# A two-layer hybrid trunk: value products in pairs of key tiles, conditioning sets without deadlines, conditioning groups placed in other gaps, own tiles in the latent chain

## The chip, the cores and the metric

The kernel runs on one core of one Trainium2 chip. The metric is the device time of one execution in microseconds (us). Before the change three runs gave 1645.55, 1646.41 and 1646.59 us (median 1646.41). Engines are called PE (TensorE), DVE (VectorE), ACT (ScalarE), POOL (GpSimd) and SP (the queue that issues most DMAs).

## The reference

Two layers (width 1024) over 256 latent and 256 context tokens. Each layer has a token-mixing half and a convolutional feed-forward half, both between RMS norms, with shift, scale and gate per feature that are computed from a conditioning vector:

```
h  = modulate(x, g0, shift, scale)        # rms_norm(x, g) * (1 + scale) + shift
A  = conv_branch(...)                     # GLU, depthwise conv 31, LayerNorm, swish
B  = window_branch(...)                   # windowed attention, 8 heads, 2 key heads
C  = retention_branch(...)                # two directions, chunks of 128
D  = global_branch(...)                   # attention with normalised q and k
y  = sum_b sigmoid(gate_b(h)) * (branch_b @ w_br[b])
x  = x + gate * rms_norm(y @ w_o)
x  = x + gate' * rms_norm(ConvFFN(modulate'(x)))
```

Attention is `p = softmax(q k^T)`, then `p v`. Latent queries see four key tiles of 128 tokens (two latent, two context), context queries the two of the context. Each layer has 12 conditioning vectors of 1024 (shift, scale and gate of both halves, in half vectors j = 0 to 11 of 512), which are `silu(c) @ ada_w + ada_b`, for latent and for context tokens (v = 0 and 1). Only the latent stream is returned, so layer 1 computes 256 columns where layer 0 computes 512.

## The kernel before

**Products.** Activations lie with features on partitions and tokens in columns. Each large product keeps single precision by splitting both sides in a high and a low part (`hh`, `hl`; `wh`, `wl`) and runs three matmuls per tile: high by high, low by high, high by low. Weights come through SP into `raw` (`NRAW` = 4 buffers); ACT casts `wh`, DVE subtracts to `wl`, and up to `NW` = 6 split units may be live.

**The order.** Nothing reorders the program later: each engine's order is what the Python code emits. A planner decides it while emitting. `Model` keeps a clock per engine and a price per operation (`Engine.us`; the one of a split matmul stands at line 110). `Flow` holds generators in streams (`chain`, `chain2`, `pv`, `main`, `aux`, `fill`, `ada`); after each group of matmuls `poll` advances those whose inputs are ready by the model's clocks and whose stream is not held back by its lag (`STREAMS`). Weight splits are one such piece (`self.weights`). `until(cond)` polls until a condition holds; where nothing can go on, it takes a step of `idle_work`, and otherwise moves the model's PE clock. Since each engine runs its own list in order, an instruction that was put early and waits holds up everything behind it on its engine.

**Value products.** `pv_gen` transposes the softmax weights of a key tile (`ptp`, four transposes), copies them (`PT`, on ACT), and multiplies with the values: `prod(kc)` is two matmuls of 64 stationary columns and 256 moving ones per key tile, which fill the two halves of the partitions of `pv`. One `prod` is emitted per key tile, each after the transposes of the next.

**Conditioning.** It is computed in two ways. `ada_gen` does a half vector on PE: eight products in fp32 (`adp`, 32 stationary columns), a copy on ACT (`adsb`), four transposes (`adt`) and a reduction on DVE. `IDLE` lists the half vectors done so in gaps: after `merge` of layer 0 four, `(0, 10), (0, 11), (1, 10), (1, 11)`; at the end of layer 0 two, `(1, 4), (1, 5)`; in layer 1 none. `ada_stream` does the others on DVE: for each feature block a multiply with reduction over 512 inputs (`adj` for the first vector of a pair, `adw` for the second), two halves. `ADA_SETS` says which half vectors, and at which stage each set begins. Two calls demand the results of a set: `flow.until(ada_need(0, 4, 5))` just before `proj_c`, and `flow.until(ada_need(0, 6, 7, 8, 9))` after the last merge. The first set begins at stage "merge D", the second at "merge A".

**The chain between the halves.** After the output projection `project` (tile `op`, copied to `ys`, squares added up in `Sy`) runs `norm_chain`: a sum over features on PE (`nrm<-ones`), `nv` on DVE, `nr` on POOL, a broadcast on PE (`nrm<-cst_sb,nr`, called R below), then `residual` (per feature block `rt` = gate times R times `ys`, `xs` += `rt`, and for the latent half `q` = square of `xs` on ACT and its sum on PE), again nv, nr, R, then `modulate` (`ht`, `hh`, `hl`). The last feature blocks of the projection are done for the latent half first, so that the latent chain (s = 0) runs beside the context half (s = 1). The tiles `rt`, `q` and `ht` share a ring of four buffers (`half_tmp`). In layer 0 `f` products follow for the latent half, then for the context half; in layer 1 there is only the latent half.

Of the kernel before, what the change touches and what calls it, by code (L numbers as in the profile page):

```python
# [14 lines left out]
D = 1024  # L15
# [12 lines left out]

IDLE = ((((0, 10), (0, 11), (1, 10), (1, 11)), ((1, 4), (1, 5))), ((), ()))

ADA_SETS = (
    ("merge D", 0, (4, 5), (0, 1)), ("merge A", 0, (6, 7, 8, 9), (0, 1)),
    ("ffn", 1, (0, 1, 2, 3), (0, 1)), ("ffn", 1, (6, 7, 8, 9), (0,)),
)
# [4 lines left out]


LEAD = 3

# [55 lines left out]
class Engine:  # L98
# [5 lines left out]
    def us(self, op, out, ins, kw):  # L104
        n = _size(out)
        if self.n == "PE":
            if op == "transpose":
                return 0.123
            if ins[0].dtype == F32R:
                return max(n, 256) / 2400 + 0.002  # L110
            if _size(ins[0]) <= 64:
                return 0.25
            return max(4 * n / 2400, 0.235)
        if self.n == "DMA":
            return max(0.1, 1.43e-3 * n)
        n = max([n] + [_size(x) for x in ins])
        psum = any(x.space == bass.MemoryType.PSUM for x in [out, *ins])
        if self.n == "ACT":
            aps = sum(1 for k in ("scale", "bias") if k in kw and hasattr(kw[k], "shape"))
            return n * 0.833e-3 + (0.05 if psum else 0.093) + 0.093 * aps + (0.06 if "accum_out" in kw else 0)  # L120
        if self.n == "POOL":
            return 0.1 + 0.14 * n
        if op == "reciprocal":
            return 0.06 + 8e-3 * n
        if op == "tensor_tensor_reduce":
            return 0.15 + 1.04e-3 * n
        aps = 0.06 if any(hasattr(kw.get(k), "shape") for k in ("scalar", "scalar1", "scalar2")) else 0
        if op in ("tensor_scalar", "tensor_copy", "memset") and not psum:
            return 0.06 + 0.52e-3 * n + aps
        return 0.065 + 1.04e-3 * n + aps  # L130
# [21 lines left out]
class Flow:  # L152
# [6 lines left out]

    STREAMS = (("chain2", 3.0, 1), ("pv", 3.0, 1), ("main", 1.5, 2), ("aux", 1.5, 1), ("fill", 0.3, 1), ("ada", 0.3, 1))  # L160

    def __init__(self, model):
        self.m = model
        self.post = []
        self.q = {s: deque() for s in ("chain", *(s for s, _, _ in self.STREAMS))}
        self.wait = {}
        self.weights = None
        self.idle_work = deque()

# [41 lines left out]
    def poll(self):  # L211
# [6 lines left out]
        did |= self.advance("chain", 5.0, 1)  # L218
        lim = 1.0 if self.q["chain"] and self.split_ahead() > 2 else 3.0
        if not self.behind(lim) and self.weights():  # L220
            did = True
# [29 lines left out]
def trunk_kernel(  # L251
# [364 lines left out]
    def ada_stream():  # L616
# [8 lines left out]
        for when, l, js, vecs in ADA_SETS:  # L625
            yield (lambda: when in stage,)
            cs = [4 * j + i for j in js for i in range(4)]
            for h in range(2):
                rows_ = [tmp("crow") for _ in vecs]
                for v, r in zip(vecs, rows_):  # L630
                    dma.dma_start(out=r, in_=c_b[:, v, 512 * h:512 * h + 512])
                raw = load(l, cs[0], h)
                for r in rows_:
# [5 lines left out]
                for n_, c in enumerate(cs):  # L639
                    cur, raw = raw, load(l, cs[n_ + 1], h) if n_ + 1 < len(cs) else None  # L640
                    for v, r in zip(vecs, rows_):
# [92 lines left out]
    def residual(l, which, s, ys, b, Sx=None, sums=None):  # L734
# [21 lines left out]
        def add(k, t):  # L756
            dve.tensor_tensor(out=xs[s][k], in0=xs[s][k], in1=t, op=ALU.add)
            if Sx is not None:
                add_sq(Sx, xs[s][k], k == 0)
            if sums is not None:  # L760
                q = half_tmp("q")
                act.activation(out=q, in_=xs[s][k], func=AF.Square)
                sq[k] = q

        for k in range(KD):
            t = half_tmp("rt")
            dve.scalar_tensor_tensor(
# [162 lines left out]
    def pv_gen(br, st, s, c, P):  # L930
# [4 lines left out]
        PT = {}  # L935

        def prod(kc):
            kt = kc + (0 if s == 0 else 2)
            for i in range(2):
# [4 lines left out]
                )  # L944

        for kc in range(nk):
            yield (avail("t"), *(P[q, i] for q in range(2) for i in range(2)))
            pt = bank("t", "ptp")
            for i in range(2):
                for q in range(2):  # L950
                    a = (2 * i + q) * 128
                    pe.transpose(pt[:, a:a + 128], P[q, i][:, kc * 128:kc * 128 + 128], ident)
            if kc:
                if pv is None:
                    yield (avail("v"), PT[kc - 1])
                    pv = bank("v", "pv")
                else:
                    yield (PT[kc - 1],)
                prod(kc - 1)
            yield (pt,)  # L960
# [3 lines left out]
        P.clear()  # L964
        yield (PT[nk - 1],)
        prod(nk - 1)
# [90 lines left out]
    def layer(l, segs):  # L1057
# [354 lines left out]
        def project(which, rh, rl, nk, ys, first, last):  # L1412
# [70 lines left out]
            def chain(s):  # L1483
                yield (lambda: got[s] == KD,)
                yield from norm_chain(l, which, s, ys, Ss[s])

            if last:
# [14 lines left out]
            for m in range(lead, KD):  # L1502
# [7 lines left out]
                else:  # L1510
                    drop()
            for m, w in held:
                p = bank("m", "op")
# [102 lines left out]
        if full:  # L1616
# [14 lines left out]
            flow.drain("aux", "main", "pv")  # L1631
            stage.add("merge D")
            merge(stD)
            flow.until(ada_need(0, 4, 5))
            proj_c()
# [16 lines left out]
        if full:  # L1652
# [3 lines left out]
            merge(stC, last=True)  # L1656
            flow.until(ada_need(0, 6, 7, 8, 9))
        else:
# [43 lines left out]
        if l == 0:  # L1702
            flow.until(ada_need(1, 0, 1, 2, 3, 6, 7, 8, 9))
            for i in IDLE[l][1]:
# [162 lines left out]
```

## Time and profile before

| | |
|---|---|
| Median of 3 runs | 1646.41 us |
| Profiled execution, its own time | 1647.13 us |
| Span of that execution | 1645.3 us |
| PE busy | 1594.7 us (97%) |
| PE weight loads busy | 1349.9 us (82%) |
| DVE busy | 1273.9 us (77%) |
| ACT busy | 796.5 us (48%) |
| Chain that ended last | PE 78%, issue 13%, DVE 5%, DMA 2%, ACT 1% |

Places, in us from the start of the span: input projections of layer 0 to 195; merges of B and D to 372; conv and retention projections (`proj_c`) 374 to 445; merges of A and C to 602; output projection to 652; gap, latent half of `f` 656 to 676; gap, context half from 685; feed-forward to 1041; gap; layer 1 from 1054: mixing to 1398, output projection to 1421, gap to 1441, feed-forward to 1636; end 1645. A row of a timeline has the start, the duration, the engine, the line, the operation with output and inputs, shapes and a count; in brackets the idle time before it and who ended it. Matmuls are pipelined: the distance of two starts says more than the duration shown.

### The profile page before, as it was taken

Reading aid. Unit: us, or ns where it says so; the run is one execution under the profiler, and the core shown is the slowest. Engines: PE = TensorE matmul, PEld = TensorE weight load, DVE = VectorE, ACT = ScalarE, POOL = GpSimd, SP = SyncE. Lnnn points to the kernel's source line nnn. Section 1 sums busy time; section 2 is a strip of 40 time slices with the busy share of each in tenths; the row PEclk is TensorE's granted clock in tenths of the full one; section 3 lists DMA queues with packets and bytes.
Section 4 is the critical chain, followed back from the end, with each engine's and each line's share of the span. In section 5 each row is a group of like instructions: output and inputs, shape, how many; then the busy total and the mean of one; then the engine's idle time right before and its main releaser. Section 6 shows DMA issues by size and latency. Waiting matters only on the chain.

```text
span 1645.3 us, 25202 instructions
## 1 busy us (share of the span) xinstructions
PE 1594.7 (97%) x9430; PEld 1349.9 (82%) x9430; DVE 1273.9 (77%) x2774; ACT 796.5 (48%) x1712; POOL 36.6 (2%) x38
## 2 busy tenths in 40 slices
PE   6999999999999999999999999899999999899998
PEld 3776776787878889888888888788688999799998
DVE  4666897999588774789788766788798976578876
ACT  3666457424432334454344333456666445466653
POOL 0000000000000000000000000000000000000000
PEclk9999999999999999999999999999999999899999
DMA  9411121234533457244544545153133435336552
GB/s 326 169 65 39 65 77 39 77 109 135 186 109 122 159 198 259 70 141 145 177 162 150 186 152 200 56 171 125 46 129 109 154 121 187 128 104 216 183 168 74
DMA packets 84282, 225.87 MB, mean 137 GB/s; under 512 B 9152, under 2 KB 18112, under 8 KB 84160
## 3 DMA queue, kind: packets, MB, share of 16 engines
q1 hardware_dynamic: 83872, 223.74, 40.8%
q8 instruction: 74, 1.21, 0.3%
q10 hardware_dynamic: 288, 0.52, 0.1%
q14 instruction: 48, 0.39, 0.1%
HBM read 223.18 MB, written 1.05 MB: 136 GB/s over the span
## 4 chain that ended last, share of the span: by engine, by line
PE 78%; issue 13%; DVE 5%; DMA 2%; ACT 1%; POOL 0%; SPq 0%; DVEq 0%; POOLq 0%; ACTq 0%
PE mg L136 16%; PE op L136 11%; PE tm L136 11%; PE mb L136 8%; PE fa L136 6%; PE fb L136 6%; PE pv L136 3%; PE sc L136 2%; PE pg L136 2%; PE pa L136 2%; PE ptp L136 2%; PE f L136 2%; PE cqk L136 1%; PE co L136 1%; PE csc L136 1%
## 5 line engine op out<-in xcount | busy, mean ns | idle before, releaser
L136 DVE TENSOR_TENSOR wl<-raw,wh 128x512 fp32r<-128x512 f32 (+1 forms) x624 | 403.7, 679 | 106.9 <-ACT wh L136 105.6
L136 ACT CAST wh<-raw 128x512 fp32r<-128x512 f32 (+1 forms) x624 | 358.1, 613 | 174.7 <-PE fb L136 46.3
L136 PE MATMUL mg<-hh,wh 128*128 128x512 f32 (+1 forms) x512 | 179.0, 350 | 0.0
L136 PE MATMUL mg<-hh,wl 128*128 128x512 f32 (+1 forms) x512 | 172.2, 336 | 0.0
L136 PE MATMUL mg<-hl,wh 128*128 128x512 f32 (+1 forms) x512 | 172.2, 336 | 0.0
L136 DVE SCALAR_TENSOR_TENSOR co<-zp,hdw,co 128x482 f32<-128x482 f32 (+29 forms) x240 | 129.9, 600 | 0.0
L136 PE MATMUL op<-gh,wh 128*128 128x256 f32 (+1 forms) x382 | 124.8, 327 | 0.0
L136 PE MATMUL op<-gh,wl 128*128 128x256 f32 (+1 forms) x382 | 123.5, 323 | 0.0
L136 PE MATMUL op<-gl,wh 128*128 128x256 f32 (+1 forms) x382 | 123.5, 323 | 0.0
L136 PE MATMUL tm<-wh,hh 128*128 128x512 f32 x272 | 112.6, 414 | 3.8 <-ACT hh L136 2.8
L136 PEld LDWEIGHTS mg<-hh,wh 128*128 128x128 f32 x512 | 97.0, 189 | 21.7 <-issue 13.4
L136 PE MATMUL tm<-wl,hh 128*128 128x512 f32 x272 | 107.7, 396 | 3.2 <-DVE wl L136 3.2
L136 PE MATMUL tm<-wh,hl 128*128 128x512 f32 x272 | 107.7, 396 | 1.8 <-DVE hl L136 1.8
L136 PEld LDWEIGHTS mg<-hh,wl 128*128 128x128 f32 x512 | 97.0, 190 | 10.3
L136 PE MATMUL fa<-hh,wh 128*128 128x256 f32 (+1 forms) x312 | 104.6, 335 | 0.0
L136 PE MATMUL fa<-hh,wl 128*128 128x256 f32 (+1 forms) x312 | 104.4, 335 | 0.0
L136 PE MATMUL fa<-hl,wh 128*128 128x256 f32 (+1 forms) x312 | 104.4, 335 | 0.0
L136 PE MATMUL fb<-hh,wh 128*128 128x256 f32 (+1 forms) x312 | 104.4, 335 | 0.0
L136 PE MATMUL fb<-hl,wh 128*128 128x256 f32 (+1 forms) x312 | 104.4, 335 | 0.0
L136 PE MATMUL fb<-hh,wl 128*128 128x256 f32 (+1 forms) x312 | 104.4, 335 | 0.0
L136 ACT ACTIVATE mth<-mg 128x512 f32<-128x512 f32 (+1 forms) x64 | 31.4, 490 | 150.2 <-PE mg L136 149.8
L136 PEld LDWEIGHTS mg<-hl,wh 128*128 128x128 f32 x512 | 97.2, 190 | 8.2
(251 smaller groups left out, 3766.0 us busy)
## 6 DMA issues: line engine op xcount, KB each, us to landing
raw<-in_w_fm SPq DMA_DIRECT2D x88, 512.0 KB, 3.5
raw<-in_f_up SPq DMA_DIRECT2D x88, 512.0 KB, 3.6
adw<-in_ada_t SPq DMA_DIRECT2D x112, 256.0 KB, 4.0
adw<-in_ada_w SPq DMA_DIRECT2D x80, 256.0 KB, 5.6
raw<-in_w_tm SPq DMA_DIRECT2D x40, 512.0 KB, 3.5
raw<-in_w_br SPq DMA_DIRECT2D x32, 512.0 KB, 3.8
raw<-in_f_d SPq DMA_DIRECT2D x32, 512.0 KB, 3.5
raw<-in_w_o SPq DMA_DIRECT2D x16, 512.0 KB, 3.9
```

The lines of the kernel that those rows point to most:

```text
L136: r = f(*a, **kw)
```

## The change

1. `pv_gen` emits the products of two key tiles together, after the transposes of the third; the last two after the loop. 2. `ADA_SETS`: the first set begins at "merge A" instead of "merge D"; both `flow.until(ada_need(0, ...))` calls are gone; the last set loses half vector (1, 6); loads run three ahead instead of one; the lag of stream `ada` goes from 0.3 to 1.0. 3. `IDLE`: (1, 10) and (1, 11) go from layer 0's middle gap to layer 1's; (1, 6) joins the end of layer 0. 4. In `residual` with sums each block has an own tile `rq`, whose first half holds the update and whose second half the square. 5. `flow.hot`: from the end of the last projection's first part until the latent chain is done, weight splits are held back while the chain or a post step is due within 0.6 us. 6. The model's price of a split matmul rises by about 0.011 us.

```diff
--- before.py
+++ after.py
@@ -26,11 +26,11 @@
 
 MERGE_ORDER = ((1, 3, 0, 2), (1, 3, 2, 0))
 
-IDLE = ((((0, 10), (0, 11), (1, 10), (1, 11)), ((1, 4), (1, 5))), ((), ()))
+IDLE = ((((0, 10), (0, 11)), ((1, 4), (1, 5), (1, 6))), (((1, 10), (1, 11)), ()))
 
 ADA_SETS = (
-    ("merge D", 0, (4, 5), (0, 1)), ("merge A", 0, (6, 7, 8, 9), (0, 1)),
-    ("ffn", 1, (0, 1, 2, 3), (0, 1)), ("ffn", 1, (6, 7, 8, 9), (0,)),
+    ("merge A", 0, (4, 5), (0, 1)), ("merge A", 0, (6, 7, 8, 9), (0, 1)),
+    ("ffn", 1, (0, 1, 2, 3), (0, 1)), ("ffn", 1, (7, 8, 9), (0,)),
 )
 NT = 60
 NRAW = 4
@@ -38,6 +38,7 @@
 NW = 6
 
 
+AHEAD = 3
 LEAD = 3
 
 
@@ -107,7 +108,7 @@
             if op == "transpose":
                 return 0.123
             if ins[0].dtype == F32R:
-                return max(n, 256) / 2400 + 0.002
+                return (max(n, 256) + 32) / 2400
             if _size(ins[0]) <= 64:
                 return 0.25
             return max(4 * n / 2400, 0.235)
@@ -157,7 +158,7 @@
 
 
 
-    STREAMS = (("chain2", 3.0, 1), ("pv", 3.0, 1), ("main", 1.5, 2), ("aux", 1.5, 1), ("fill", 0.3, 1), ("ada", 0.3, 1))
+    STREAMS = (("chain2", 3.0, 1), ("pv", 3.0, 1), ("main", 1.5, 2), ("aux", 1.5, 1), ("fill", 0.3, 1), ("ada", 1.0, 1))
 
     def __init__(self, model):
         self.m = model
@@ -165,6 +166,7 @@
         self.q = {s: deque() for s in ("chain", *(s for s, _, _ in self.STREAMS))}
         self.wait = {}
         self.weights = None
+        self.hot = False
         self.idle_work = deque()
 
     def now(self):
@@ -217,6 +219,8 @@
                     self.post.remove(g)
         did |= self.advance("chain", 5.0, 1)
         lim = 1.0 if self.q["chain"] and self.split_ahead() > 2 else 3.0
+        if self.hot and self.split_ahead() > 0 and (self.soon("chain", 0.6) or any(self.there(g, 0.6) for g in self.post)):
+            lim = -9.0
         if not self.behind(lim) and self.weights():
             did = True
         for s, lim, width in self.STREAMS:
@@ -629,7 +633,7 @@
                 rows_ = [tmp("crow") for _ in vecs]
                 for v, r in zip(vecs, rows_):
                     dma.dma_start(out=r, in_=c_b[:, v, 512 * h:512 * h + 512])
-                raw = load(l, cs[0], h)
+                raw = deque(load(l, c, h) for c in cs[:AHEAD])
                 for r in rows_:
                     yield (r,)
                     th = tmp("crth")
@@ -637,7 +641,9 @@
                     yield (th,)
                     dve.scalar_tensor_tensor(out=r, in0=th, scalar=1.0, in1=r, op0=ALU.add, op1=ALU.mult)
                 for n_, c in enumerate(cs):
-                    cur, raw = raw, load(l, cs[n_ + 1], h) if n_ + 1 < len(cs) else None
+                    cur = raw.popleft()
+                    if n_ + AHEAD < len(cs):
+                        raw.append(load(l, cs[n_ + AHEAD], h))
                     for v, r in zip(vecs, rows_):
                         yield (cur, r)
                         o = ada[l][:, c, v:v + 1]
@@ -758,12 +764,17 @@
             if Sx is not None:
                 add_sq(Sx, xs[s][k], k == 0)
             if sums is not None:
-                q = half_tmp("q")
+                q = both[k][:, 256:512]
                 act.activation(out=q, in_=xs[s][k], func=AF.Square)
                 sq[k] = q
 
+        both = {}
         for k in range(KD):
-            t = half_tmp("rt")
+            if sums is None:
+                t = half_tmp("rt")
+            else:
+                both[k] = tmp("rq")
+                t = both[k][:, 0:256]
             dve.scalar_tensor_tensor(
                 out=t, in0=ys[k][:, half(s)], scalar=gain[l][:, (1, 3)[which], k, s:s + 1], in1=R,
                 op0=ALU.mult, op1=ALU.mult,
@@ -943,6 +954,10 @@
                     PT[kc][:, 256 * i:256 * i + 256], start=(kc == 0), stop=(kc == nk - 1),
                 )
 
+        def prods(kcs):
+
+            yield (avail("v"), *(PT[kc] for kc in kcs)) if pv is None else tuple(PT[kc] for kc in kcs)
+
         for kc in range(nk):
             yield (avail("t"), *(P[q, i] for q in range(2) for i in range(2)))
             pt = bank("t", "ptp")
@@ -950,19 +965,20 @@
                 for q in range(2):
                     a = (2 * i + q) * 128
                     pe.transpose(pt[:, a:a + 128], P[q, i][:, kc * 128:kc * 128 + 128], ident)
-            if kc:
-                if pv is None:
-                    yield (avail("v"), PT[kc - 1])
-                    pv = bank("v", "pv")
-                else:
-                    yield (PT[kc - 1],)
-                prod(kc - 1)
+            if kc == 2:
+                yield from prods((0, 1))
+                pv = bank("v", "pv")
+                prod(0)
+                prod(1)
             yield (pt,)
             PT[kc] = tmp("PT")
             act.copy(PT[kc], pt)
             free(pt)
         P.clear()
-        yield (PT[nk - 1],)
+        yield from prods((nk - 2, nk - 1))
+        if pv is None:
+            pv = bank("v", "pv")
+        prod(nk - 2)
         prod(nk - 1)
         yield (pv,)
         yh, yl = st["yh"][c][:, half(s)], st["yl"][c][:, half(s)]
@@ -1483,6 +1499,8 @@
             def chain(s):
                 yield (lambda: got[s] == KD,)
                 yield from norm_chain(l, which, s, ys, Ss[s])
+                if s == 0:
+                    flow.hot = False
 
             if last:
                 hready.clear()
@@ -1509,6 +1527,8 @@
                     held.append((m, w))
                 else:
                     drop()
+            if last and not end:
+                flow.hot = True
             for m, w in held:
                 p = bank("m", "op")
                 chunks([(p, w)], rh, rl, half(1), nk)
@@ -1629,9 +1649,7 @@
             go("main", *attention("D", stD, segs))
             merge(stB, first=True)
             flow.drain("aux", "main", "pv")
-            stage.add("merge D")
             merge(stD)
-            flow.until(ada_need(0, 4, 5))
             proj_c()
             go("main", ret_start(), *(ret_gen(h) for h in range(4)))
         else:
@@ -1654,7 +1672,6 @@
             merge(stA, there=lambda: not flow.q["fill"])
             flow.drain("main")
             merge(stC, last=True)
-            flow.until(ada_need(0, 6, 7, 8, 9))
         else:
             merge(stC, there=lambda: not flow.q["main"])
             merge(stA, last=True, there=lambda: not flow.q["fill"])
@@ -1700,7 +1717,7 @@
                     down(gi - 1, ys)
         flow.drain("aux")
         if l == 0:
-            flow.until(ada_need(1, 0, 1, 2, 3, 6, 7, 8, 9))
+            flow.until(ada_need(1, 0, 1, 2, 3, 7, 8, 9))
             for i in IDLE[l][1]:
                 flow.idle_work.append(ada_gen(*i, ada_load(*i)))
         down(2, ys)
```

**PE, merges of layer 0.** `mg` is the gate product of a merge, `pv` the value products, `sc` scores of the next head pair. Before:

```order
L136 MATMUL mg<-hh,wh 128x512
L136 MATMUL mg<-hl,wh 128x512
L136 MATMUL mg<-hh,wl 128x512
L136 MATMUL pv<-PT,kv 64x256 x2
L136 MATMUL mg<-hh,wh 128x512
L136 MATMUL mg<-hl,wh 128x512
L136 MATMUL mg<-hh,wl 128x512
L136 MATMUL pv<-PT,kv 64x256 x2
L136 MATMUL mg<-hh,wh 128x512
L136 MATMUL mg<-hl,wh 128x512
L136 MATMUL mg<-hh,wl 128x512
L136 MATMUL ptp<-cst_sb,P 128x128 x4
```

The same stretch of the merge after the change:

```order
L137 MATMUL mg<-hh,wh 128x512
L137 MATMUL mg<-hl,wh 128x512
L137 MATMUL mg<-hh,wl 128x512
L137 MATMUL pv<-PT,kv 64x256 x4
L137 MATMUL mg<-hh,wh 128x512
L137 MATMUL mg<-hl,wh 128x512
L137 MATMUL mg<-hh,wl 128x512
L137 MATMUL ptp<-cst_sb,P 128x128 x4
L137 MATMUL sc<-KT,QT 128x256 x8
```

Two bursts of two matmuls have become one of four, and the transposes of the tiles stand by themselves.

**DVE, conv and retention projections (`proj_c`) of layer 0.** `adj` and `adw` are the reductions of the first conditioning set, the rows with `ada_93 128x1` read the sum, `wl` are the low parts of the weights of `proj_c`, `CG` its gate. Before, the end of the set and what follows:

```order
L136 ISA adw,ada_93<-adw,crow,ada_93 128x512
L136 ISA ada_93 128x1
L136 SCALAR_TENSOR_TENSOR gain_95<-ada_93,vec_sb 128x8
L136 TENSOR_TENSOR wl<-raw,wh 128x512 x22
L136 SCALAR_TENSOR_TENSOR CG<-cth,tm 128x512
```

After the change, the rows there:

```order
L137 SCALAR_TENSOR_TENSOR av<-ath,av 128x512
L137 SCALAR_TENSOR_TENSOR yAl<-av,yAh 128x512
L137 TENSOR_TENSOR wl<-raw,wh 128x512 x16
L137 SCALAR_TENSOR_TENSOR CG<-cth,tm 128x512
L137 TENSOR_TENSOR CG<-CG,gn 128x512
L137 SCALAR_TENSOR_TENSOR CG<-cth,tm 128x512
```

The 32 reductions of that set, which all stood ahead of the 22 `wl` before, now stand among the merges of A and C.

**PE, middle gap of layer 1.** `op` is the end of the output projection, `nrm` the norm's sums (from `Sy`, then from `q` or `rq`) and broadcasts (from `nr`), `xtp` transposes of `xs` for the end of the kernel, `f` the first products behind the gap. Before:

```order
L136 MATMUL op<-ah,wh 128x256
L136 MATMUL op<-al,wh 128x256
L136 MATMUL op<-ah,wl 128x256
L136 MATMUL nrm<-ones,Sy 128x1 x2
L136 MATMUL nrm<-cst_sb,nr 128x128 x2
L136 MATMUL nrm<-ones,q 128x1 x16
L136 MATMUL xtp<-cst_sb,xs 128x128 x4
L136 MATMUL nrm<-cst_sb,nr 128x128 x2
L136 MATMUL f_14378<-hh,wh 128x256
L136 MATMUL f_14378<-hl,wh 128x256
```

After the change:

```order
L137 MATMUL op<-ah,wl 128x256
L137 MATMUL adp<-adw,cS 32x512 x4
L137 MATMUL nrm<-ones,Sy 128x1 x2
L137 MATMUL adp<-adw,cS 32x512 x4
L137 MATMUL nrm<-cst_sb,nr 128x128 x2
L137 MATMUL adp<-adw,cS 32x512 x8
L137 MATMUL nrm<-ones,rq 128x1 x12
L137 MATMUL adt<-cst_sb,adsb 128x128 x4
L137 MATMUL nrm<-ones,rq 128x1 x4
L137 MATMUL adt<-cst_sb,adsb 128x128 x4
L137 MATMUL nrm<-cst_sb,nr 128x128 x2
L137 MATMUL f_14350<-hh,wh 128x256
```

The sixteen products and eight transposes of two conditioning half vectors stand in the gap, between the chain's steps; the `xtp` have gone behind the first `f` products.

## Rows read from the trace of the kernel before

**Rows 1.** The page, part 1: busy time, share of span, count of instructions.

```profile
PE 1594.7 (97%) x9430; PEld 1349.9 (82%) x9430; DVE 1273.9 (77%) x2774; ACT 796.5 (48%) x1712; POOL 36.6 (2%) x38
```

**Rows 2.** Timeline of PE in merge D of layer 0: a value burst.

```profile
235.43 0.40 PE L136 MATMUL mg<-hh,wl 128*128 128x512 f32 x1
235.76 0.65 PE L136 MATMUL pv<-PT,kv 128*64 128x256 f32 x4
...
236.68 0.39 PE L136 MATMUL mg<-hl,wh 128*128 128x512 f32 x1
236.91 0.39 PE L136 MATMUL mg<-hh,wl 128*128 128x512 f32 x1
```

**Rows 3.** Tile pv: duration min/median/max in ns, first and last start.

```profile
L136 PE MATMUL pv<-PT,kv x320: 379/404/431, 113.9 to 1264.8; 128*64 128x256 f32 x160
```

**Rows 4.** Timeline of PE, start of the kernel: conditioning products of 256 columns.

```profile
32.37 1.07 PE L136 MATMUL adp<-adw,cS 128*32 128x256 f32 x16 [0.27 <-DVE ada L136]
...
39.09 0.64 PE L136 MATMUL adp<-adw,cS 128*32 128x256 f32 x8
```

**Rows 5.** Timeline of DVE in proj_c of layer 0: two of the reductions.

```profile
405.41 0.75 DVE L136 CUSTOM_DVE_ANT_0 adj<-adw,crow,ada 128x512 f32<-128x512 f32 x1
...
406.88 0.75 DVE L136 CUSTOM_DVE_ANT_0 adj<-adw,crow,ada 128x512 f32<-128x512 f32 x1
```

**Rows 6.** Timeline of PE in proj_c of layer 0.

```profile
407.19 0.39 PE L136 MATMUL tm<-wh,hh 128*128 128x512 f32 x1
...
410.75 0.79 PE L136 MATMUL tm<-wl,hh 128*128 128x512 f32 x1 [3.18 <-DVE wl L136]
...
414.25 0.39 PE L136 MATMUL tm<-wh,hh 128*128 128x512 f32 x1
```

**Rows 7.** Windows: busy us (instructions) of each engine, clock, DMA share, GB/s.

```profile
445.00:602.00 157.00, 156.19 (x735) 126.12 (x733) 131.82 (x308) 52.10 (x92) 4.93 (x4) 1.00 0.41 139
1329.00:1332.00 3.00, 3.00 (x15) 3.00 (x16) 1.32 (x5) 0.38 (x1) 0.70 (x1) 0.50 0.00 0
1421.00:1441.00 20.00, 11.80 (x48) 10.30 (x48) 11.85 (x28) 6.21 (x15) 1.77 (x2) 0.59 0.33 114
```

**Rows 8.** Timeline of PE, middle of layer 0.

```profile
654.33 0.71 PE L136 MATMUL nrm<-cst_sb,nr 128*128 128x128 f32 x4 [0.98 <-POOL nr L136]
...
656.15 0.38 PE L136 MATMUL f<-hh,wh 128*128 128x256 f32 x1 [1.11 <-ACT hh L136]
...
676.31 2.78 PE L136 MATMUL adp<-adw,cS 128*32 128x512 f32 x24
...
685.14 0.39 PE L136 MATMUL f<-hh,wh 128*128 128x256 f32 x1 [1.11 <-ACT hh L136]
...
705.80 1.03 PE L136 MATMUL adt<-cst_sb,adsb 128*128 128x128 f32 x8
...
709.88 0.49 PE L136 MATMUL fa<-hh,wh 128*128 128x512 f32 x1
```

**Rows 9.** Timeline of PE and ACT, end of layer 0.

```profile
1053.76 1.11 PE L136 MATMUL adt<-cst_sb,adsb 128*128 128x128 f32 x4 [3.86 <-ACT adsb L136]
...
1053.14 0.56 ACT L136 COPY adsb<-adp 128x512 f32<-128x512 f32 x1
```

**Rows 10.** Timeline of ACT and DVE, middle of layer 1.

```profile
1421.19 1.14 ACT L136 CAST wh<-raw 128x512 fp32r<-128x512 f32 x2
...
1427.97 0.47 DVE L136 SCALAR_TENSOR_TENSOR rt<-ys,gain,nrm 128x256 f32<-128x256 f32 x1
...
1434.64 0.48 DVE L136 SCALAR_TENSOR_TENSOR rt<-ys,gain,nrm 128x256 f32<-128x256 f32 x1 [0.44 <-PE nrm L136]
```

**Rows 11.** Timeline of DVE, middle of layer 0: the same step beside the projection.

```profile
642.51 0.48 DVE L136 SCALAR_TENSOR_TENSOR rt<-ys,gain,nrm 128x256 f32<-128x256 f32 x1
...
644.21 0.48 DVE L136 SCALAR_TENSOR_TENSOR rt<-ys,gain,nrm 128x256 f32<-128x256 f32 x1
```

**Rows 12.** Timeline of PE, end of retention in layer 1.

```profile
1328.31 0.30 PE L136 MATMUL cyt<-cst_sb,cy 128*128 128x128 f32 x1 [2.17 <-DVE cy L136]
```

## The prediction

> **What bounds the kernel now.** I read the page's first part: PE is busy 97% of the span, DVE 77% [rows 1]. So time can only go by less PE work per result, or by closing the few stretches where PE waits or runs at half clock. I looked for these with the timeline of PE, stage by stage, from waits to what they leave behind: a wait costs twice, because the granted clock falls behind it. In [rows 6] PE waits for a low half of weights between 407.19 and 410.75, then needs until 414.25 for eight products (0.44 each) that elsewhere start 0.23 apart [rows 2]. The windows view confirms it where retention ends in layer 1 (clock 0.50, that is 1.2 of 2.4 GHz) and in layer 1's middle gap (0.59) [rows 7].
>
> **Value bursts.** In [rows 2] the stream product before a burst starts at 235.43, the second one behind it at 236.68: 1.25 us for two stream products at 0.23 and the burst, so 0.79 for two matmuls (four rows). Their 0.65 from first start to last end, less the 0.40 that one lasts [rows 3], puts the two halves 0.25 apart; 0.50 of the 0.79 is work, 0.29 is paid once per burst. There are 320 rows of value products [rows 3], 80 bursts. The order after has 40 bursts of twice the size, so 40 are saved: 40 x 0.29 = 11.6 us. The nearest other row: conditioning products of the same 256 columns, sixteen rows 1.07 against eight 0.64 [rows 4]; 0.43 for what a second key tile adds would give 40 x 0.36 = 14.4. The other end is nothing, if each key tile pays its own entry. I take 11.6, from the row of the operation itself.
>
> These bursts use 64 stationary columns between products of 128. The Trainium skill (TensorEngine Tiling (Array Packing), Key Properties under Tiling Modes) says that changing the tiling mode drains the engine while changing the tile within a mode does not. By it the fixed part is paid once per burst and the sum keeps the 11.6; if each pair of tiles drained by itself, the term would be 0, a rival below. No row of before has a value burst of four, so the trace leaves that open.
>
> **The first conditioning set.** Before, its 32 reductions stand in front of the weight halves of the retention projection, demanded by the call ahead of it. Two take 406.88 - 405.41 = 1.47, so 0.735 each [rows 5]. PE pays 410.75 - 407.19 - 0.23 = 3.33 for the wait and 3.50 - 8 x 0.23 = 1.66 for the half clock [rows 6]: 5.0 us. In the order after no reduction stands there. Bounds: 5.0 if the wait goes, 0 if the next late thing (casts, weights) takes its place; I take 5.0, since PE waits there for DVE alone.
>
> These reductions go into the merges of A and C: the order has 84 there, 56 before, so 28 x 0.735 = 20.6 us more. DVE is busy 131.8 of the 157 us there [rows 7], which leaves 25.2: it fits, with 4.6 to spare, and PE has no slack in it (156.2 busy). Since no call demands the results at once any more, a reduction can be put where the model sees DVE ahead. Cover gone would mean late weight halves. Bounds 0 and +6 (a wait as in [rows 6] with its half clock, once); I take +2.
>
> **Middle of layer 0.** Four things. (a) The latent chain's broadcast R now stands twelve products ahead of the projection's end; before it came at 654.33 [rows 8], some two us behind it (the list of places has its end at 652), so with twelve products at 0.12 and its own length the chain is some 4 us earlier. (b) But the weight splits are held back until the chain is done, and on ACT the copy of the conditioning product stands behind all eight `hh`, with the transposes on PE waiting for it ahead of `f`. That pattern is in the trace at the end of layer 0: 3.86 us of waiting [rows 9]. The chain's gain is therefore lost on its way to `f` and `f` starts later by about as much: +4.0. (c) The gap ahead of the context half, 676.31 to 685.14 = 8.8 us [rows 8], holds sixteen products of conditioning and transposes between the chain's steps; they are gone from there, and the context chain runs ahead while `f` waits. I leave 4 us for the norm and the modulation: -4.8. (d) The conditioning burst at 705.80 to 709.88 goes: -4.1. Sum -4.9; -8.9 if the held splits cost nothing, +4 if the gap refills.
>
> **End of layer 0.** One half vector more. Its copy (0.56, [rows 9]) and four transposes stand behind the `hh`, +1.0, and three splits stand before the first `ht`, +0.5: +1.5. Bounds -2 (the copies now come in two parts, the first early) and +4 (a second wait like 3.86).
>
> **Middle of layer 1.** From the third to the eighth `rt`, 1427.97 to 1434.64, five steps take 6.67 us, each waiting for PE to release one of four shared buffers [rows 10]. With own tiles the step is as beside the projection in layer 0, 1.70 for two [rows 11]; 5 x 0.85 = 4.25, so -2.4. The last square of `ys` stands behind two casts of 1.14 [rows 10], which are now held back: -1.1. The conditioning products fill PE's idle time between the chain's steps; if they hold the clock, the broadcasts and sums go at full speed, worth about 1.0 (a broadcast of four rows 0.71 in [rows 8], and the window's clock is 0.59 [rows 7]). The four transposes of `xs` that leave the gap now cost PE time in the stream: half of the eight transposes in 1.03 at 705.80 [rows 8], +0.5, less a little of the gap they leave: +0.4. Sum -4.1. Late results are the other bound: sixteen products at 24 rows in 2.78 [rows 8] (two rows each) are 3.7 us, 7.4 at half clock, beside a gap of 20: +3 if half of that lands on the chain or on their loads, which SP now issues ahead of the feed-forward's weights. -8 if all of PE's half clock goes.
>
> Here the skill speaks against the change: TensorE: Matmul & The Clock Gate (Part 4: PE-mode transpose) says that transposes don't count as PE being busy. By it the eight transposes ahead of `f` hold nothing, the 1.0 is lost and the term is -3.1. The trace shows a gap with transposes and broadcasts before 685.14 [rows 8], without telling transposes apart.
>
> **End of retention, layer 1.** PE waits 2.17 for DVE at 1328.31 [rows 12], then three us at clock 0.50 [rows 7], half of them lost: 3.7. Before, the product that needs these transposes stands right behind; after, 132 instructions lie between. I take -3.7; bounds -5 and +3 (the transposes wait elsewhere).
>
> **Sum.** -11.6 - 5.0 + 2.0 - 4.9 + 1.5 - 4.1 - 3.7 = -25.8. The profiled execution took 1647.13 (span 1645.3), so 1621.3; the median of the runs lies 0.7 below it, 1620.6. I say 1621.
>
> **Rivals.** *Bursts give nothing* (each key tile pays its 0.79): 1621.3 + 11.6 = 1633. For it: no row shows four in a burst. Against: eight more conditioning rows in one burst cost 0.43 and not 0.64 [rows 4]. *The gaps don't close*: chains in the three gaps and the end of retention find another late step, and only bursts and the first set stay: 1647.1 - 11.6 - 5.0 + 2.0 = 1632.5. For it: each gap ends in a wait of 1.11 for `hh` [rows 8] that nothing changes, and every chain still goes through POOL. *DVE binds the merges of A and C* and the kernel is slower: each added reduction delays a weight half, PE waits 20.6 us and half as much again goes at half clock, as 1.66 followed 3.33 in [rows 6]: 30.9 instead of 2.0. The rest is -27.8, so +3.1: 1650. It decides from 18.5 us of waits on. Against it stand the 25.2 idle us of DVE [rows 7]; for it, that they come in pieces, and that the order is fixed by a model. *Both of the first two at once*: 1632.5 + 11.6 = 1644, which can't be told from no change.
>
> **Numbers.** Forecast 0.56 (own range 1612 to 1630), gaps stay 0.20, bursts nothing 0.13, both 0.05, slower 0.06. The measurement can tell 0.2% (3.3 us) from no change. Faster 0.89, same 0.05, slower 0.06. The unknown bounds below (14.4 for the bursts, -8.9 and -8 for the gaps) reach 1611 without all meeting; above, both middle rivals with some loss reach 1638. Range 1611 to 1638.
>
> **What would show it.** Value bursts of four whose distance between the stream products around them is about 1.3 us net, not 1.58; no wait of PE for `wl` and full clock in the retention projection; DVE some 152 busy of 157 in the merges of A and C with PE still without waits; `rt` steps of 0.85 in layer 1 instead of 1.3; the context half of `f` within 5 us behind the latent one; no burst of 4 us behind it. Wrong would be waits for `wl` in the merges beyond 5 us in sum, a conditioning copy that holds `f` by over 6 us, or bursts of four at twice the price.

## The result, and the profile after

The changed kernel takes 1627.91 us (median; 1625.57 to 1629.71), the kernel before 1646.5 in the same runs: ratio 0.9887, interval 0.987 to 0.9904, 18.6 us faster. The forecast was 1621 with a range of 1611 to 1638: direction and range held, the gain was 7 us smaller. The profiled execution of after took 1629.71 (span 1627.9, 17.4 shorter than before). The page's first part of after, against [rows 1]:

```profile
PE 1583.5 (97%) x9450; PEld 1356.1 (83%) x9450; DVE 1263.4 (78%) x2762; ACT 791.1 (49%) x1711; POOL 35.8 (2%) x38
```

By stage, from PE's timelines (from the start of the last product of one stage to that of the next, so the gap ahead of a stage counts with it):

| Stretch | before | after | difference |
|---|---|---|---|
| start to the end of merges B and D | 372.0 | 364.1 | -7.9 |
| conv and retention projections, with the gap ahead | 72.6 | 67.1 | -5.4 |
| merges of A and C | 157.8 | 168.7 | +10.9 |
| output projection | 49.6 | 51.1 | +1.5 |
| gap, `f`, to the last product ahead of the first `op` of the feed-forward | 133.9 | 130.1 | -3.8 |
| rest of layer 0, its end gap, layer 1's first projection | 294.5 | 293.7 | -0.8 |
| from there to the end of layer 1's merges | 317.1 | 307.7 | -9.4 |
| output projection, middle gap, the 480 products of `f`, `fa`, `fb` | 104.4 | 101.7 | -2.7 |

The first stretch differs by itself between profiles: after, e10 and e12, whose program for PE is the same up to there, have 363.3 to 365.2. Two things stand out: nearly every term has the forecast's sign, and one stage gave 10.9 us back. PE's timeline of after at a value burst, to be held against [rows 2]:

```profile
231.47 0.40 PE L137 MATMUL mb<-yh,wl 128*128 128x512 f32 x1
231.79 1.08 PE L137 MATMUL pv<-PT,kv 128*64 128x256 f32 x8
232.81 0.50 PE L137 MATMUL mg<-hh,wh 128*128 128x512 f32 x1
233.14 0.40 PE L137 MATMUL mg<-hl,wh 128*128 128x512 f32 x1
```

233.14 - 231.47 = 1.67 us with the burst, less two stream products at 0.23: 1.21 for four products (eight rows), where two bursts of two cost 1.58.

The retention projection, where PE had waited 3.3 us and run slowly [rows 6], is full (windows view of after: PE busy 43.00 of 43.00, clock 1.00):

```profile
388.00:431.00 43.00, 43.00 (x191) 35.63 (x190) 12.85 (x21) 13.06 (x24) 0.00 (x0) 1.00 0.34 115
```

The merges of A and C are not. Windows view of after, then of before, of this stage (span, busy us and counts of PE, weight loads, DVE, ACT, POOL, clock, DMA share, GB/s):

```profile
431.50:600.00 168.50, 160.90 (x737) 129.59 (x735) 148.35 (x358) 51.79 (x96) 5.15 (x4) 0.98 0.47 155
```

```profile
444.80:602.60 157.80, 156.99 (x737) 126.81 (x737) 132.62 (x309) 52.27 (x93) 4.93 (x4) 1.00 0.41 138
```

PE has 7.6 us without work where it had 0.8, with the same 737 rows; DVE still has 20 us free. So DVE is not full, but late. PE's timeline of after, the waits of this stage:

```profile
441.69 1.14 PE L137 MATMUL csc<-CQK 64*128 64x256 f32 x8
...
447.00 1.13 PE L137 MATMUL csc<-CQK 64*128 64x256 f32 x4
...
450.15 1.05 PE L137 MATMUL co<-tmo,scD 128*128 128x128 f32 x8
...
454.05 0.71 PE L137 MATMUL co<-tmo,scD 128*128 128x128 f32 x4 [2.84 <-DVE scD L137]
...
491.01 1.95 PE L137 MATMUL co<-tmo,scD 128*128 128x128 f32 x16
...
507.59 0.33 PE L137 MATMUL cyt<-cst_sb,cy 128*128 128x128 f32 x1 [3.11 <-DVE cy L137]
```

The score products `csc` of the chunk come in bursts, two of them at 441.69 and 447.00; `co` waits 2.84 for the decayed scores `scD`, later `cyt` 3.11 for `cy`, and behind each wait stream products start 0.43 apart instead of 0.23: half clock. DVE's timeline of after shows why they are late:

```profile
441.88 0.49 DVE L137 TENSOR_TENSOR E<-E,cst_sb 128x128 f32<-128x128 f32 x2
...
448.16 0.69 DVE L137 SCALAR_TENSOR_TENSOR scD<-csc,E 128x512 f32<-128x512 f32 x1 [5.79 <-PE csc L137]
...
486.15 0.68 DVE L137 SCALAR_TENSOR_TENSOR crow<-crth,crow 128x512 f32<-128x512 f32 x1
...
492.55 0.75 DVE L137 CUSTOM_DVE_ANT_0 adj<-adw,crow,ada 128x512 f32<-128x512 f32 x1 [5.71 <-PE co L137]
```

DVE stands idle for 5.79 and for 5.71 us, each time for PE. The second of these rows decides how to read both: a reduction `adj` reads loads and earlier sums, nothing that PE writes, yet it waits for PE's `co` (the burst at 491.01). It can only wait for its own buffer. All these tiles share one pool of 60 buffers (`NT`), and a tile takes one whose last reader has been emitted, run or not; in the built program that `adj` has the buffer of an `scD` which `co` still reads, and the `scD` of the first row, whose scores were done with the burst at 441.69, has the buffer of a `CQK` tile that the last `csc`, at 447.00, still reads. `tmp` takes buffers without telling the planner who held them, so the planner's model knows nothing of such waits.

### The profile page after: what moved, and what is told of

Read it like the earlier page. It is cut to its first block, busy times and chain, and to the rows that moved or that the text cites. A ratio compares the mean times of both kernels' runs of the same rounds, so it can differ in the third digit from the quotient of the medians.

```text
span 1627.9 us, 25230 instructions
## 1 busy us (share of the span) xinstructions
PE 1583.5 (97%) x9450; PEld 1356.1 (83%) x9450; DVE 1263.4 (78%) x2762; ACT 791.1 (49%) x1711; POOL 35.8 (2%) x38
## 3 DMA queue, kind: packets, MB, share of 16 engines
q8 instruction: 74, 1.21, 0.3%
## 4 chain that ended last, share of the span: by engine, by line
PE 75%; issue 13%; DVE 8%; DMA 2%; ACT 1%; SPq 0%; POOL 0%; DVEq 0%; POOLq 0%; ACTq 0%
PE mg L137 15%; PE op L137 11%; PE tm L137 11%; PE mb L137 7%; PE fa L137 6%; PE fb L137 6%; PE f L137 2%; PE pv L137 2%; PE pa L137 2%; PE pg L137 2%; PE sc L137 2%; PE ptp L137 2%; DVE wl L137 2%; PE cqk L137 1%; DMA adw<-in_ada_w 1%
## 5 line engine op out<-in xcount | busy, mean ns | idle before, releaser
L137 DVE TENSOR_TENSOR wl<-raw,wh 128x512 fp32r<-128x512 f32 (+1 forms) x624 | 404.0, 680 | 104.4 <-ACT wh L137 103.5
```

Source lines behind the costliest of these rows:

```text
L137: r = f(*a, **kw)
```

## The experiments

Times are medians, before 1646.0 to 1646.4 in each group of runs. "A and C" is the length of those merges in the run's profile, from their first product to their last (157.6 before, 168.5 after).

| Run | Time | Ratio to before, interval | A and C | loads ahead |
|---|---|---|---|---|
| e1_bursts_only | 1639.37 | 0.9957, 0.9943 to 0.997 | 157.7 | 1 |
| e2_no_bursts | 1642.28 | 0.9978, 0.9968 to 0.9988 | 169.5 | 3 |
| e3_deadlines_back | 1633.72 | 0.9923, 0.991 to 0.9935 | 167.1 | 3 |
| e4_early_no_deadline | 1625.80 | 0.9877, 0.9863 to 0.989 | 168.6 | 3 |
| e5_before_bursts_lag | 1638.01 | 0.9947, 0.9935 to 0.996 | 155.8 | 1 |
| e6_before_bursts_price | 1634.96 | 0.9926, 0.9914 to 0.9939 | 158.4 | 1 |
| e7_lag_back | 1633.37 | 0.9921, 0.9907 to 0.9934 | 159.1 | 1 |
| e8_lag_back_early | 1615.16 | 0.981, 0.9797 to 0.9823 | 156.1 | 1 |
| e9_one_ahead_early | 1616.35 | 0.9822, 0.9809 to 0.9836 | 157.8 | 1 |
| e10_no_hold | 1622.70 | 0.9857, 0.9844 to 0.9871 | 168.3 | 3 |
| e11_best_no_hold | 1610.40 | 0.9784, 0.9769 to 0.9798 | 156.1 | 1 |
| e12_shared_ring | 1638.47 | 0.9954, 0.9941 to 0.9966 | 169.0 | 3 |

### What the bursts are worth

**e1_bursts_only** is the kernel before with the new `pv_gen`, **e2_no_bursts** the changed kernel with the old one.

```diff
 # e1: before with
-            if kc: ... prod(kc - 1)
+            if kc == 2: yield from prods((0, 1)); ...; prod(0); prod(1)
 # e2: the same, undone in after
```

> The kernel before with the value products in bursts of two key tiles and nothing else of the change. In the profile after, a burst of four products costs 1.22 us net where two bursts of two cost 2 x 0.79. Theory: 40 bursts saved at 0.36 each, -14.4 us against the kernel before, about 1632. The forecast's size (0.29 each, -11.6): 1635. Rival, that the bursts only shift the waits of softmax: 1643 or more.

> The changed kernel with one value product per key tile as before. Theory: the 14.4 us come back, about 1642. Rival, that part of the saving belongs to the other edits (a merge that runs with fewer interruptions meets its weights late): 1634 or less.

Taken from the changed kernel the bursts cost 1642.3 - 1627.9 = 14.4, as the theory had it. Put into the kernel before they brought only 6.8. PE's timeline of e1 shows where the rest stayed:

```profile
365.26 1.03 PE L136 MATMUL atp<-cst_sb,co 128*128 128x128 f32 x8
...
372.32 3.78 PE L136 MATMUL abc<-cst_sb,arr 128*128 128x128 f32 x16 [6.03 <-POOL arr L136]
...
375.76 0.77 PE L136 MATMUL cqk<-hh,wh 128*128 128x512 f32 x1
```

The merge of D, now shorter, ends before the conv branch's norm is done: PE waits 6.03 us for it, then starts `cqk` at half clock. The gap ahead of that projection is 10.7 us here, 2.4 before, 1.0 after the whole change. In part it is made good at once: DVE catches up meanwhile (the first set's reductions end 3.6 us earlier than before), the wait for `wl` of [rows 6] is gone without any edit to the conditioning, and the projections take 66.1 us instead of 70.2. So 14.4 is the worth of the bursts only where what stands ahead of the next stage is early too; e6 below shows which part of the change brings that about.

### What slows the merges of A and C

**e3_deadlines_back** and **e4_early_no_deadline** are the changed kernel with the first set begun at merge D again, e3 with both deadlines, e4 without.

```diff
-    ("merge A", 0, (4, 5), (0, 1)),
+    ("merge D", 0, (4, 5), (0, 1)),
+            stage.add("merge D")          # ahead of merge(stD)
+            flow.until(ada_need(0, 4, 5)) # e3 only, and the one for 6 to 9
```

> The changed kernel with the first conditioning set begun at merge D again and both deadlines in place (loads three ahead and the lag stay as changed). Theory: the merges of A and C, which took 168.5 us after against 157.7 before, are slowed by the reductions that stand between the retention's steps on DVE; with the set gone from there they take 157 to 160, and the retention projection pays about 5 again: about 1622 to 1624, faster than the changed kernel. Rival, that the merges are slow because the planner's new price or lag places the retention's products worse: merges stay at 168, about 1632.

> The changed kernel with the first conditioning set begun at merge D again, but without the deadlines: its reductions fill DVE's free time from merge D on. Theory: merges of A and C 157 to 160 us and no wait in the retention projection: about 1618. Rival (the planner's price or lag): merges stay at 168, about 1628. A third: DVE's reductions delay weight halves in the conv and retention projections without a deadline too: about 1622.

The theory fell: with 64 reductions in the stage (56 before the change, 79 in the changed kernel) it still took 167.1 and 168.6. The deadlines cost 7.9 us between e3 and e4, and the wait for `wl` goes with them and not with the set's place: the projections take 70.3 us in e3, 66.9 in e4. What was left were the lag, the price and the loads ahead, which I had not named.

**e5_before_bursts_lag** and **e6_before_bursts_price** are e1 with one of the planner's numbers each; **e7_lag_back** and **e8_lag_back_early** are the changed kernel and e4 with the lag and the loads as before.

```diff
 # e5: e1 with                            # e6: e1 with
-("ada", 0.3, 1)                          -max(n, 256) / 2400 + 0.002
+("ada", 1.0, 1)                          +(max(n, 256) + 32) / 2400
 # e7: after, e8: e4, each with
-AHEAD = 3                                -("ada", 1.0, 1)
+AHEAD = 1                                +("ada", 0.3, 1)
```

> The kernel before with the value bursts (1639.4 alone) and the lag of stream ada at 1.0 instead of 0.3. The first set with or without its deadline left the merges of A and C at 167 to 169 us, so neither its reductions nor its place slows them. Theory: the lag does; with it reductions are emitted while the model sees DVE up to 1.0 us ahead of PE, so they stand in front of the retention's decay products on DVE. Merges of A and C 166 to 169, about 1648. Rival (the price of a split matmul): they stay at 158, about 1639.

> The kernel before with the value bursts and the new price of a split matmul, lag 0.3. Theory (the lag): merges of A and C 157 to 160, about 1639. Rival (the price): 166 to 169, about 1648.

> The changed kernel with the lag at 0.3 and one conditioning load ahead, as before the change; sets, price, gaps, hold and tiles stay. Theory (the lag): the merges of A and C fall from 168.5 towards 158, fewer reductions fit in there, and the kernel takes about 1618. Rival (the price): 168 and 1628. A third, that the reductions which no longer fit in land where the output projection's chain needs DVE: 158, but 1624 or more.

> The changed kernel with the lag at 0.3, one load ahead, and the first set begun at merge D without deadlines (1625.8 with the lag at 1.0). Theory: merges of A and C near 158, no wait in the retention projection: 1615 to 1617. Rival (the price): 1626.

Neither number slows the stage by itself (155.8, 158.4). But e6 answers what e1 left open. PE's timeline of e6 where e1 waited 6.03 us:

```profile
365.40 1.95 PE L136 MATMUL abc<-cst_sb,arr 128*128 128x128 f32 x16
367.10 0.48 PE L136 MATMUL cqk<-hh,wh 128*128 128x512 f32 x1
```

With the new price added to e1, and nothing else, PE no longer waits for the norm, the gap ahead of the projection is 1.9 us, and the kernel is 4.4 us faster than e1, though the wait for `wl` is back (3.7 in the waits view). So the sixth edit, for which the forecast has no term, carries part of the bursts' gain.

e7 and e8 heal the stage (159.1, 156.1). They changed two things together, though, lag and loads. e8 is 10.6 us faster than e4. e7 is no gain: with the stage healed its conditioning comes too late for the middle gap of layer 0 (ten reductions stand on DVE between 661.3 and 669.4 us, ahead of the `ht` that `f` needs), the waits view of PE there having (wait in total, times, longest):

```profile
PE nrm L137 <- DVE Sx L137: 13.1, 1, 13.1
PE f L137 <- ACT hh L137: 5.4, 1, 5.4
```

**e9_one_ahead_early** separates lag and loads: e4 with one load ahead, lag at 1.0.

```diff
-AHEAD = 3
+AHEAD = 1
```

> The changed kernel with the first set begun at merge D without deadlines, one load ahead, and the lag left at 1.0: the fast variant (1615.2) with only the lag as changed. Theory (the lag together with the new price slows the retention): merges of A and C 167 to 169, about 1626. Rival (the three loads ahead did it): 156 to 159, about 1616.

The rival is right: 1616.35, the stage at 157.8. Windows view and DVE's timeline of e4, then of e9, for the same stage:

```profile
430.90:599.60 168.70, 162.80 (x737) 130.32 (x736) 138.68 (x328) 52.22 (x93) 5.46 (x4) 0.97 0.40 134
```

```profile
441.25 0.48 DVE L137 TENSOR_TENSOR E<-E,cst_sb 128x128 f32<-128x128 f32 x2
...
447.54 0.69 DVE L137 SCALAR_TENSOR_TENSOR scD<-csc,E 128x512 f32<-128x512 f32 x1 [5.81 <-PE csc L137]
...
490.59 0.75 DVE L137 CUSTOM_DVE_ANT_0 adj<-adw,crow,vec_sb 128x512 f32<-128x512 f32 x1 [4.26 <-PE co L137]
```

```profile
432.10:590.00 157.90, 156.82 (x737) 126.73 (x736) 138.67 (x328) 52.24 (x93) 5.25 (x4) 1.00 0.42 143
```

```profile
442.53 0.48 DVE L137 TENSOR_TENSOR E<-E,cst_sb 128x128 f32<-128x128 f32 x2
...
443.50 0.69 DVE L137 SCALAR_TENSOR_TENSOR scD<-csc,E 128x512 f32<-128x512 f32 x1 [0.50 <-PE csc L137]
```

The DVE instructions up to that `scD` are the same in both and in the same order; DVE's busy time in the stage is 138.7 in both. What differs is the wait, 5.81 against 0.50, and the one of 4.26 ahead of `adj`, which e9 has not. In the built program of e4 this `scD` has the buffer of a `CQK` tile and waits for the last `csc` that reads it; in that of e9 its buffer was last held by an `E` tile, and it waits for its own scores alone. All six programs with three loads ahead have stages of 167 to 170, and in each DVE waits 5.7 or 5.8 for `csc` and 4.3 to 6.0 for `co` ahead of a reduction; all seven with one load, and the kernel before, have 156 to 159 and no wait of DVE for PE there over 2.1. That three loads ahead cause it is shown; that they do it through the buffers (more of the 60 taken early, so that a tile of the retention gets one that PE still reads) is read from the traces and the built programs. More buffers with three loads ahead were not tried.

### The hold and the own tiles

**e10_no_hold** is the changed kernel with `flow.hot` never set, **e11_best_no_hold** the same with e8, **e12_shared_ring** the changed kernel with `half_tmp` in `residual`.

```diff
-                flow.hot = True
+                flow.hot = False          # e10, e11
-                both[k] = tmp("rq")
+            t = half_tmp("rt")            # e12
```

> The changed kernel without the hold on weight splits during the chain. Before, the first f product came 4.1 us after the output projection, now 9.5, with 2.6 of waiting for the conditioning copy. Forecast's theory: the hold costs 4 there, so without it f starts 4 to 5 us earlier; what is behind it (the context half's gap, the conditioning in the feed-forward) takes back 2 to 4: kernel 0 to 3 us faster, layer 1's gap unchanged at 16 to 17. Rival: the hold is what shortens the context half's gap and layer 1's gap: kernel 3 to 6 us slower.

> The fast variant (lag 0.3, one load ahead, first set from merge D, no deadlines; 1615.2) without the hold. By the forecast's theory 1612 to 1615, by the rival 1618 to 1621.

> The changed kernel with the four shared buffers for update and square as before. Theory: the steps of layer 1's middle gap wait for the buffers again, 2.4 us, so the gap is 19 to 20 against 16.7 and the kernel 2 to 5 us slower, layer 0's middle included. Rival: with the conditioning products in the gap PE's clock is up and the sums free the buffers in time: gap 16.7 to 17.5, kernel within 1.5 us.

Without the hold the kernel is 5.2 us faster, and e8 4.8, which makes e11 the fastest here: 1610.40, 2.2% under the kernel before. PE's timeline of e10, the middle of layer 0:

```profile
651.41 0.28 PE L137 MATMUL op<-ah,wl 128*128 128x256 f32 x1
...
651.83 0.38 PE L137 MATMUL f<-hh,wh 128*128 128x256 f32 x1
...
670.62 1.92 PE L137 MATMUL adp<-adw,cS 128*32 128x512 f32 x16
```

`f` starts 0.4 us behind the projection instead of 9.5; the conditioning products stand in the gap ahead of the context half, which is 8.9 us again instead of 3.5, and by the first `fa` 3.5 of the 9.1 us are given back. The end of layer 0, where the hold works too, is 3.1 shorter without it. Layer 1's gap is 17.9 without the hold, 16.7 with it: there the hold earns 1.2.

e12 is inconclusive in its total. Layer 1's gap is 18.4 (16.7 with own tiles), so the tiles earn about 1.7, less than the theory's 2.4. Most of the 10.6 us lie elsewhere: the stretch from the feed-forward's first `op` to layer 1's first projection is 8.4 longer, since its order starts that projection without split weights (waits of PE there, same columns as above):

```profile
PE pa L137 <- DVE wl L137: 4.5, 2, 3.8
PE pa L137 <- ACT wh L137: 2.6, 1, 2.6
```

The moved groups of `IDLE` were not run by themselves; what is said of them below is read from the trace of the changed kernel alone.

## Why the prediction was right, and where its size failed

**Value bursts, -11.6 forecast, -14.4 measured.** Right in kind. The second key tile costs 1.21 - 0.79 = 0.42, the 0.43 of the conditioning rows [rows 4], and not the 0.50 I took from one burst's own rows; so each burst saved is worth 0.36 in the median and not 0.29. In e1, with the bursts alone, layer 1's mixing takes 311.4 us instead of 317.1: 5.7 for 16 bursts. The rule of the Trainium skill (TensorEngine Tiling (Array Packing), Key Properties) agrees with this as far as it was used: the fixed part is paid once per burst, whatever the number of key tiles in it.

**First set, -5.0 forecast, -5.4 measured** over the projections with their gap, 4.1 of it in the projections, where the wait stood. Dropping the deadline does it, not the later start: e4 begins the set at merge D as before and has no wait for `wl`. Both deadlines together are worth 7.9 (e3 against e4).

**Merges of A and C, +2 forecast, +10.9 measured.** This is the term that failed, and more than the whole error of 7. I counted DVE's busy time against its free time, 20.6 us of reductions into 25.2. DVE's busy time rose by 15.7, for 79 reductions in the stage and not 84, so it did fit; but that was beside the point, for with only 64 (e4) the stage is as slow. The edit that costs is the one I gave no price, "loads run three ahead", by two waits of DVE for buffers, in a stage that had no slack on PE [rows 7]. Of the signs named ahead, "PE still without waits" failed, with 7.4 us of waits in the stage; none of them is for `wl`, the wait that was to show the forecast wrong. The rival that DVE binds these merges was near it in its place and in the half clock behind each wait, and wrong in its cause: not the reductions' own time. That the sum stayed as near as 7 us is partly luck: the bursts came out 2.8 and the end of layer 0 2.3 better than forecast, against 8.9 lost here.

**Middle of layer 0, -4.9 forecast, -3.8 measured** with the stretch to the feed-forward. The parts of PE's timeline of after, against [rows 8]:

```profile
651.08 0.28 PE L137 MATMUL op<-ah,wl 128*128 128x256 f32 x1
...
651.29 3.64 PE L137 MATMUL adp<-adw,cS 128*32 128x512 f32 x32
...
657.50 1.14 PE L137 MATMUL adt<-cst_sb,adsb 128*128 128x128 f32 x8 [2.58 <-ACT adsb L137]
...
660.58 0.56 PE L137 MATMUL f<-hh,wh 128*128 128x256 f32 x1
...
681.01 0.28 PE L137 MATMUL f<-hh,wl 128*128 128x256 f32 x1
...
684.48 0.58 PE L137 MATMUL f<-hh,wh 128*128 128x256 f32 x1 [1.11 <-ACT hh L137]
```

`f` starts 9.5 us behind the projection, 5.4 later than before (forecast +4.0); the transposes wait 2.58 for the copy that stands behind all `hh` on ACT. The hold is what does it: without it (e10) `f` starts 0.4 us behind the projection and the stretch to the feed-forward gives 9.4, near the bound of -8.9 that I had for held splits that cost nothing. The gap ahead of the context half is 3.5 (forecast 4). The burst at 705.80 is gone.

**End of layer 0, +1.5 forecast, -0.8 measured** with the feed-forward. PE's timeline of after, against [rows 9]:

```profile
1039.06 4.50 PE L137 MATMUL adp<-adw,cS 128*32 128x512 f32 x40
...
1045.27 0.66 PE L137 MATMUL adt<-cst_sb,adsb 128*128 128x128 f32 x4 [1.71 <-ACT adsb L137]
...
1047.66 1.14 PE L137 MATMUL adt<-cst_sb,adsb 128*128 128x128 f32 x8 [1.40 <-ACT adsb L137]
...
1049.93 0.56 PE L137 MATMUL pg<-hh,wh 128*128 128x256 f32 x1
```

Forty rows of conditioning stand where PE had waited anyway, and the single wait of 3.86 has become 1.71 and 1.40.

**Middle of layer 1, -4.1 forecast, -3.9 measured** for the gap (20.7 to 16.7; 1.3 lost again in `f`). DVE's, then PE's timeline of after, against [rows 10]:

```profile
1411.95 0.47 DVE L137 SCALAR_TENSOR_TENSOR rq<-ys,gain,nrm 128x256 f32<-128x256 f32 x1
...
1414.86 0.47 DVE L137 SCALAR_TENSOR_TENSOR rq<-ys,gain,nrm 128x256 f32<-128x256 f32 x1
...
1419.08 0.16 DVE L137 TENSOR_SCALAR nv<-nrm 128x2 f32<-128x2 f32 x1 [3.07 <-PE nrm L137]
```

```profile
1405.68 0.28 PE L137 MATMUL op<-ah,wl 128*128 128x256 f32 x1
...
1411.85 4.74 PE L137 MATMUL nrm<-ones,rq 128*128 128x1 f32 x24
1416.45 1.09 PE L137 MATMUL adt<-cst_sb,adsb 128*128 128x128 f32 x4
1417.34 1.71 PE L137 MATMUL nrm<-ones,rq 128*128 128x1 f32 x8
...
1420.07 1.22 PE L137 MATMUL nrm<-cst_sb,nr 128*128 128x128 f32 x4
...
1422.40 0.58 PE L137 MATMUL f<-hh,wh 128*128 128x256 f32 x1 [1.11 <-ACT hh L137]
```

The windows view, with the clock of two halves of the gap (0.5 is 1.2 of 2.4 GHz):

```profile
1406.00:1414.00 8.00, 6.88 (x53) 3.23 (x52) 5.70 (x15) 3.48 (x8) 1.09 (x1) 1.00 0.60 205
1414.50:1422.00 7.50, 6.72 (x30) 5.99 (x29) 2.77 (x11) 2.31 (x7) 0.70 (x1) 0.50 0.00 0
```

The steps take 0.73 us instead of 1.3, faster than the 0.85 forecast (-3.0 for the five instead of -2.4), and end three us before `nv`. But the clock falls among PE's sums of single columns, ahead of the transposes; the last broadcast takes 1.22 as before. Of the 1.0 put on the clock only the first broadcast's part came (0.71 instead of 1.23). So the size came out near the forecast by another split, more from the steps and less from the clock. The rule of the Trainium skill on transposes (TensorE: Matmul & The Clock Gate, Part 4: PE-mode transpose), by which the term was -3.1, is neither borne out nor refuted here, since the clock fell ahead of them.

**End of retention, -3.7 forecast, -3.7 measured**: layer 1's mixing takes 307.7 us, and 311.4 in e1, which has the bursts alone. PE's timeline of after, against [rows 12]:

```profile
1300.44 0.33 PE L137 MATMUL cyt<-cst_sb,cy 128*128 128x128 f32 x1 [0.26 <-DVE cy L137]
...
1300.53 0.36 PE L137 MATMUL mg<-hh,wh 128*128 128x256 f32 x1
```

The wait of 2.17 is 0.26 and the product behind it is at full clock. With the 5.7 of the bursts of layer 1 that makes the 9.4 of the table.

## What to carry to other kernels

A pool of shared buffers is a queue that no planner sees unless it is modelled: taking loads further ahead can delay a tile of another chain by its buffer, on an engine that has time to spare. A wait of an instruction for an engine whose results it does not read is the sign, and it is in one row of the timeline. And an edit's worth depends on what is late next: the bursts gave 6.8 us alone, 11.4 with the planner's new price (e6), and 14.4 beside the rest.

## What the runs showed of the hardware

Among stream products of 512 columns, two fp32 value products of 64 stationary columns cost 0.79 us (median of 17 bursts before), four cost 1.22 (median of 10 after): 0.36 is paid once per burst. Broadcasts of 128 stationary columns, taken the same way, show no such part: eight rows cost 0.89 (after, at 364.35), sixteen 1.79 (e6, at 365.40).
